# SBUF tiles on multiples of 256 bytes, and every row of the first norm weighted by one VectorE instruction, in a hybrid decoder layer

## The chip, the cores and the metric

The kernel runs on one core of one Trainium2 chip. The metric is the time of the program on the device, in microseconds (us), as the median of several runs. The engines are named as in the profile: PE is TensorE (PEld its weight loads), DVE is VectorE, ACT is ScalarE, POOL is GpSimd, SP issues most DMAs. SBUF is the core's working memory, 128 partitions wide; an address here is the byte offset within a partition, and a tile's *residue* is its address modulo 256.

## The reference

One decoder layer over 1024 tokens of width 1024, in float32. What matters here:

```
n = rmsnorm(x, mix_norm_w)                 # x * rsqrt(mean(x*x) + eps) * w, row by row
p = n @ w_in                               # columns: z | x B C | dt | q | k | v
y_s = gated SSD scan of (z, xBC, dt)       # convolution, chunked scan, silu(z) gate
y_a = differential attention of (q, k, v)
h = x + concat(y_s, y_a) @ w_out
h = h + (silu(n2 @ w_gate) * (n2 @ w_up)) @ w_down,  n2 = rmsnorm(h)
out = rmsnorm(h)
```

## The kernel before

**Products.** A large product is made of three PE passes: each operand is split into a high part (rounded to float32r by ACT) and a low part (the rest, by DVE), in `split` (L170 to L176) for weights and in `norm_transpose` (L113 to L124) for the normed rows. `mm3` (L126 to L129) issues hi\*hi, hi\*lo and lo\*hi into one PSUM tile, so each step of a product is three matmuls on lines 127, 128 and 129. The first operand of a matmul is the stationary one (its 128 columns are loaded as weights), the second the moving one (it streams through, 256, 264 or 512 columns here).

**First norm.** The 1024 tokens are eight blocks of 128 rows, t = 0 to 7. For each, `norm_rows` (L94 to L111) lets ACT square the row and sum it up (L99), DVE makes the mean (`ms_n`, L89), POOL raises it to the power -0.5 (`rs_n`, L91), and then the row is weighted: for even t by one DVE instruction with two SBUF tensors and a column (L111: x times rs times the norm's weight `mixw`); for odd t, POOL multiplies x by `mixw` (L108) and ACT scales it by `rs` (L109). PE then transposes the block in two halves of four (L120, `pt_n`, two PSUM buffers in pool SC), ACT rounds each half to `nhi` (L123), and DVE subtracts to get `nlo` (L124). A later transpose into the same PSUM buffer waits for that subtraction.

**First product.** `gate_dt` projects the 16 columns of dt and the first 512 of the gate z in two passes of 264 columns (a = 0 and 1; `proj_z0`, L258 to L266). Each pass has its weights in two units of four blocks of 128 rows, `wr_z` (as loaded), `wh_z` and `wl_z` (its parts), [128, 4, 264]. `wr` has two buffers, `wh` and `wl` three each, all in pool `wp`, in slots as large as the largest tile of each: 4 * 264 * 4 = 4,224 bytes, which is 16.5 times 256.

**Placement.** Pools follow one another in SBUF: `const` (its last tile is `pcol`, 69 columns), `small`, `big` (`nhi`, `nlo`, later operands), `wp`, `a4`, `p4`, `hx`, `ob`, `cv`, `sp`. In the built program `big` begins at 18,144, which is 224 modulo 256. From there on each tile's size is a multiple of 256 except in `wp`, so that `big`, `a4`, `p4`, `hx`, `ob` and `cv` are all at residue 224. The eight slots of `wp` alternate: `wr` 224 and 96, `wh` 224, 96, 224, `wl` 96, 224, 96. Every big tile is thus at 32 modulo 64.

**Order.** The kernel is recorded by a tile framework whose scheduler orders the instructions of each engine and inserts the waits; only one stretch of the FFN has its PE order fixed by hand. SP's loads are issued in its order, and each that reuses a buffer waits for that buffer's last reader.

**What follows.** After the first product: the projections with 512 moving columns (`proj_T`: B, C, x, q and k, 28 of them, each two halves of 24 matmuls), the SSD scans, attention, the output projection (256 columns), gate and up (11 pairs of column tiles, two matrices, seven products of 12 matmuls each; the stationary parts `wa` are in the `wh` and `wl` slots), and the down projection (11 pairs of row tiles, seven products of 12 matmuls; there both the stationary `dg` and the moving `dw` are in those slots).

Of the kernel before, what the change touches and what calls it, by code (L numbers as in the profile page):

```python
# [9 lines left out]
F32 = mybir.dt.float32  # L10
F32R = mybir.dt.float32r
# [6 lines left out]
P = 128  # L18
# [6 lines left out]
def tile_hybrid_block(  # L25
# [56 lines left out]
    nc.vector.memset(mhalf, -0.5)  # L82
    pcol = const.tile([P, 69], F32, name="pcol")
    CW, CB, SN, SL = 0, 48, 60, 68
# [9 lines left out]
    def norm_rows(parts, wbc, outs, name, pool=(), junk=None):  # L94
        """outs = RMSNorm of the row whose column pieces are parts; pieces in pool are weighted on Pool and scaled on ACT"""
        n, w = len(parts), DM // len(parts)
        ss = small.tile([P, n], F32, tag="ss1", name="ss_" + name)
        for i, p in enumerate(parts):
            nc.scalar.activation(outs[i] if junk is None else junk, p, AF.Square, accum_out=ss[:, i:i + 1])  # L99
        if n > 1:  # L100
            s1 = small.tile([P, 1], F32, tag="ss1", name="st_" + name)
            nc.vector.tensor_tensor(s1, ss[:, 0:1], ss[:, 1:2], op=ALU.add)
            ss = s1
        r = rstd_of(ss, DM, name)
        for i, (p, o) in enumerate(zip(parts, outs)):
            wi = wbc[:, i * w:i * w + w]
            if i in pool:
                nc.gpsimd.tensor_tensor(o, p, wi, op=ALU.mult)  # L108
                nc.scalar.mul(o, o, r)  # L109
            else:  # L110
                nc.vector.scalar_tensor_tensor(o, p, r, wi, op0=ALU.mult, op1=ALU.mult)  # L111
# [51 lines left out]

# [1 line left out]
    def load_raw(src, shape, name):  # L165
# [12 lines left out]
    w_in_k = w_in2.rearrange("(k p) c -> p k c", p=P)  # L178

    def z0_raw(a, u):  # L180
        """columns of dt and of the gate of group 0: 264 of 528"""
        raw = wp.tile([P, 4, 264], F32, tag="raw", bufs=2, name=f"wr_z0_{a}_{u}")
        k = slice(4 * u, 4 * u + 4)
        if a == 0:
            nc.sync.dma_start(raw[:, :, 0:16], w_in_k[:, k, C_DT:C_DT + 16])
            nc.sync.dma_start(raw[:, :, 16:264], w_in_k[:, k, C_Z:C_Z + 248])
        else:
            nc.sync.dma_start(raw, w_in_k[:, k, C_Z + 248:C_Z + 512])
        return raw

    def z0_unit(raw, a, u):
        hi = wp.tile([P, 4, 264], F32R, tag="wh", bufs=3, name=f"wh_z0_{a}_{u}")
        lo = wp.tile([P, 4, 264], F32R, tag="wl", bufs=3, name=f"wl_z0_{a}_{u}")
        split(hi, lo, raw)
        return hi, lo

# [1 line left out]
    xs = []  # L198
    mixw = P4([P, DM], F32, "mixw")
    for t in range(NT):  # L200
        xt = A4([P, DM], F32, f"x_{t}")
        nc.sync.dma_start(xt, x2[t * P:(t + 1) * P, :])
        xs.append(xt)
        if t == 0:
            nc.sync.dma_start(mixw, mix_norm_w[0].partition_broadcast(P))
        if t == 2:
            zraw = [z0_raw(0, u) for u in range(2)]
    nhi = [B16([P, KD, 512], f"nhi{i}") for i in range(2)]
    nlo = [B16([P, KD, 512], f"nlo{i}") for i in range(2)]
    for t in range(NT):  # L210
        norm_transpose([xs[t]], mixw, nhi, nlo, t, (CV if t % 2 else P4)([P, DM], F32, f"xm_{t}"), SC, f"n{t}",
                       (0,) if t % 2 else ())
        if t == 2:
            zus = [z0_unit(zraw[u], 0, u) for u in range(2)]

# [1 line left out]
    prow = P4([69, P], F32, "prow")  # L217
# [5 lines left out]
    nc.tensor.transpose(pps, prow, ident[:69, :69])  # L223
    nc.vector.tensor_copy(pcol, pps)
    nc.vector.tensor_scalar(pcol[:, SL:SL + 1], pcol[:, SL:SL + 1], 1.0 - LAMBDA_INIT, None, op0=ALU.mult)
# [9 lines left out]

# [1 line left out]
    def w_unit(src, shape, name, alloc=None):  # L237
# [10 lines left out]
    def proj_T(*jobs):  # L248
        """each job: a weight, a column, a name and sink(half, psum [128 columns, 512 tokens])"""
        us = [w_unit(w_k[:, :, col:col + P], [P, KD, P], name) for w_k, col, name, _ in jobs]  # L250
        for half in range(2):
            for (hi, lo), (_, _, name, sink) in zip(us, jobs):
                ps = MM([P, 512], f"mm_{name}_{half}")
                for k in range(KD):
                    mm3(ps, hi[:, k, :], lo[:, k, :], nhi[half][:, k, :], nlo[half][:, k, :], k == 0, k == KD - 1)
                sink(half, ps)

    def proj_z0(us, name, sink):  # L258
        """units of 264 columns; sink(t, psum [128 tokens, 264])"""
        for t in range(NT):  # L260
            ps = (MS if t % 4 > 1 else MM)([P, 264], f"mm_{name}_{t}")
            tk = slice((t % 4) * P, (t % 4) * P + P)
            for k in range(KD):
                hi, lo = us[k // 4]
                mm3(ps, nhi[t // 4][:, k, tk], nlo[t // 4][:, k, tk], hi[:, k % 4, :], lo[:, k % 4, :],
                    k == 0, k == KD - 1)  # L266
            sink(t, ps)

    def proj_nat(col, name, sink):
        """256 columns; sink(t, psum [128 tokens, 2 blocks from t, 256])"""  # L270
        us = [w_unit(w_in_k[:, 4 * u:4 * u + 4, col:col + 256], [P, 4, 256], f"{name}_{u}") for u in range(2)]
# [9 lines left out]

# [1 line left out]
    W16 = [P, NT, 16]  # L283
# [49 lines left out]

# [1 line left out]
    def conv_tiles(*tiles):  # L335
# [21 lines left out]
    def gate_dt():  # L357
        """the gate of group 0 and dt"""
        for a in range(2):
            zt = [None]  # L360
            w0, w = (0, 248) if a == 0 else (248, 264)

            def sink(t, ps):
                if t % 2 == 0:
                    zt[0] = CV([P, 2, w], F32, f"zt0_{a}_{t}")
                if a == 0:
                    nc.vector.tensor_tensor(adt[:, t, :], ps[:, 0:16], hv[:, 0, :], op=ALU.add)
                nc.scalar.activation(zt[0][:, t % 2, :], ps[:, 264 - w:], AF.Silu)
                if t % 2 == 1:
                    nc.gpsimd.dma_start(z_d[t - 1:t + 1, :, w0:w0 + w].rearrange("t p c -> p t c"), zt[0])  # L370
            proj_z0(zus if a == 0 else [z0_unit(z0_raw(1, u), 1, u) for u in range(2)], f"z0_{a}", sink)

# [138 lines left out]

# [1 line left out]
    cneg = sp.tile([P, P], F32, tag="cs", name="cneg")  # L513
# [13 lines left out]
    def v_pair(hh):  # L527
        # [head][block] views of the two heads; in the last pair but one, the heads' tiles are freed one by one
        by_head = hh == NH // 2 - 2
# [129 lines left out]

# [1 line left out]
    KG = 4  # L661
# [14 lines left out]
    def out_block(t, kys, ws, name, bank=MM):  # L676
        """two token blocks from t, 256 columns"""
        ps = bank([P, 2, 256], f"po_{name}_{t}")
# [47 lines left out]

# [1 line left out]
    # gate and up by Winograd's seven products: A are two column tiles by two halves of the contraction, B the two  # L728
    # halves of the contraction by two halves of the tokens; C = A B is summed up in PSUM (X, Y and Z)
    ORDER = (1, 2, 6, 5, 7, 3, 4)  # L730
# [4 lines left out]
    def room(p, early):  # L735
        """an operand B: [hi or lo][block of 128 rows] views of 512 tokens"""
        if early:
# [59 lines left out]
    def ffn_pair(pr, raws, order=ALL, ybank=SC):  # L797
        """silu(gate) * up of two column tiles; they and their sums as operands of the down projection to g_d"""
        sg, tm, c22, reg, sm = {}, {}, {}, [{}, {}], [{}, {}]
# [145 lines left out]
    def final_half(t, nh, last):  # L945
        """the first half of a row to be ready is weighted before its scale is known"""
        ho = h_parts(ho_all, t)
# [12 lines left out]

    # down, by the same seven products: A are the two halves of the tokens by two row tiles, B the row tiles by two
    # halves of the columns
    SLOT = {2: 0, 4: 1, 1: 2, 7: 3, 5: 4, 6: 5, 3: 6}
# [28 lines left out]
    for gi, prs in enumerate(groups):  # L992
# [5 lines left out]
        def psums(two, name):  # L998
            """four banks: one for each block of 128 tokens of a half"""
            if two:  # L1000
# [81 lines left out]
```

## Time and profile before

| What | Value |
|---|---|
| Median of 3 runs | 1642.38 us (1641.95 to 1642.83) |
| Profiled execution, span | 1643.3 us |
| PE busy | 1597.2 us (97%), 9170 matmuls |
| DVE busy | 1071.6 us (65%) |
| ACT busy | 775.8 us (47%) |
| POOL busy | 429.2 us (26%) |
| PE's first instruction | 8.33 us after the span's start |

The profile is of one execution; no time of its own is listed for that execution beside its span. The span lies 0.9 us above the median of the runs, so differences are worked out on the span and taken off the median. In a row of the timeline the columns are start, duration, engine, line, operation, and output<-inputs; matmuls are pipelined, so their pace is read from the starts, not from the durations.

### The profile page before, as it was taken

What the parts mean: (1) busy time and instruction counts of PE and PEld (TensorE: products, weight loads), DVE (VectorE), ACT (ScalarE), POOL (GpSimd) and SP (SyncE); (2) the same over time, 40 slices, a digit from 0 to 9 for tenths busy, and PEclk for the clock granted to TensorE, in tenths of its full rate; (3) what the DMA queues carried; (4) which work ended last, traced back from release to release, by engine and by line L of the source; (5) the groups of instructions that cost most, each with busy time, mean ns of one, the idle gap of its engine ahead of it and who ended that gap; (6) DMA issues with size and microseconds to landing.
All of it is one profiled execution on the core that took longest, in us unless ns stands there. A gap on an engine that the chain in (4) does not pass through costs nothing. (4 is left out here: it accounts for less than half of the span.)

```text
span 1643.3 us, 23716 instructions
## 1 busy us (share of the span) xinstructions
PE 1597.2 (97%) x9170; PEld 1386.9 (84%) x9170; DVE 1071.6 (65%) x1682; ACT 775.8 (47%) x1608; POOL 429.2 (26%) x378
## 2 busy tenths in 40 slices
PE   6999999999999999999999998999999999999997
PEld 6988878887989989889999987888888888778885
DVE  5345745688776676677674477455555555898987
ACT  6444764456555565575552245333333333334445
POOL 4100330032000000013300034444444443542322
PEclk9999999999999999999999999999999999999999
DMA  5321451143011110147523221233333323944122
GB/s 195 110 79 52 129 163 56 36 142 92 24 46 39 46 33 27 45 130 229 162 77 116 84 99 56 96 102 104 111 116 118 98 96 134 365 166 186 39 103 103
DMA packets 105291, 172.78 MB, mean 105 GB/s; under 512 B 7813, under 2 KB 75530, under 8 KB 103770
## 3 DMA queue, kind: packets, MB, share of 16 engines
q1 hardware_dynamic: 95210, 137.11, 25.2%
q0 software_dynamic: 9968, 34.15, 6.3%
q8 instruction: 72, 1.18, 0.3%
q14 instruction: 41, 0.34, 0.1%
HBM read 125.82 MB, written 45.42 MB: 104 GB/s over the span
## 5 line engine op out<-in xcount | busy, mean ns | idle before, releaser
L127 PE MATMUL x<-n,wa 128*128 128x512 f32 x352 | 138.7, 396 | 0.0
L128 PE MATMUL x<-n,wa 128*128 128x512 f32 x352 | 138.7, 394 | 0.0
L129 PE MATMUL x<-n,wa 128*128 128x512 f32 x352 | 137.8, 394 | 0.0
L590 ACT ACTIVATE p<-s,nmx 128x256 f32<-128x256 f32 (+7 forms) x128 | 94.4, 740 | 53.2 <-DVE nmx L588 49.9
L172 ACT CAST wa<-s 128x512 fp32r<-128x512 f32 x88 | 54.7, 622 | 132.3 <-PE x L129 59.4
L173 DVE TENSOR_TENSOR wa<-s,wa 128x512 fp32r<-128x512 f32 x88 | 76.8, 873 | 51.1 <-ACT wa L172 50.8
L172 ACT CAST dg<-gd 128x512 fp32r<-128x512 f32 x77 | 47.7, 620 | 114.7 <-PE dx L129 57.2
L588 DVE TENSOR_REDUCE nmx<-s 128x1 f32<-128x256 f32 (+7 forms) x128 | 95.3, 754 | 2.4
L173 DVE TENSOR_TENSOR dg<-gd,dg 128x512 fp32r<-128x512 f32 x77 | 66.2, 862 | 23.3 <-ACT dg L172 23.2
L129 PEld LDWEIGHTS x<-n,wa 128*128 128x128 f32 x352 | 66.5, 189 | 15.1
L128 PEld LDWEIGHTS x<-n,wa 128*128 128x128 f32 x352 | 66.6, 189 | 14.8
L127 PEld LDWEIGHTS x<-n,wa 128*128 128x128 f32 x352 | 66.6, 189 | 14.8
L127 PE MATMUL mm_z<-wh_z,nhi 128*128 128x264 f32 (+1 forms) x256 | 75.9, 298 | 2.3 <-ACT wh_z L172 2.3
L611 PE MATMUL o<-v,p 128*128 128x128 f32 x576 | 77.7, 275 | 0.0
L129 PE MATMUL mm_z<-wh_z,nlo 128*128 128x264 f32 (+1 forms) x256 | 77.3, 303 | 0.0
L611 PEld LDWEIGHTS o<-v,p 128*128 128x128 f32 x576 | 73.5, 191 | 2.7
L128 PE MATMUL mm_z<-wl_z,nhi 128*128 128x264 f32 (+1 forms) x256 | 75.0, 294 | 0.0
L127 PE MATMUL mm_v<-wh_v,nhi 128*128 128x256 f32 x256 | 74.2, 290 | 0.0
L129 PE MATMUL mm_v<-wh_v,nlo 128*128 128x256 f32 x256 | 74.1, 290 | 0.0
L128 PE MATMUL mm_v<-wl_v,nhi 128*128 128x256 f32 x256 | 73.5, 287 | 0.0
L128 PE MATMUL po_a<-wl_wo,yh 128*128 128x256 f32 x256 | 72.6, 283 | 0.0
L91 POOL TENSOR_TENSOR rs_o<-ms_o,mhalf 128x4 f32<-128x4 f32 x16 | 18.0, 1125 | 208.4 <-DVE ms_o L89 208.3
(331 smaller groups left out, 5172.9 us busy)
## 6 DMA issues: line engine op xcount, KB each, us to landing
gd<-g_d SPq DMA_DIRECT2D x11, 1792.0 KB, 7.8
wr_g<-in_w_gate_dram SPq DMA_DIRECT2D x22, 512.0 KB, 3.8
wr_u<-in_w_up_dram SPq DMA_DIRECT2D x22, 512.0 KB, 4.3
g_d<-sg SPq DMA_DIRECT2D x22, 512.0 KB, 5.1
wr_d<-in_w_down_dram SPq DMA_DIRECT2D x22, 512.0 KB, 5.0
L<-cs_d POOLq DMA_DIRECT2D x16, 512.0 KB, 4.4
wr_y<-yT_d SPq DMA_DIRECT2D x16, 512.0 KB, 3.8
wr_wo<-in_w_out_dram SPq DMA_DIRECT2D x16, 512.0 KB, 3.5
```

What stands on the lines that cost most here:

```text
L91: nc.gpsimd.tensor_tensor(r, ms, mhalf[:, :w], op=ALU.pow)
L127: nc.tensor.matmul(ps, lh, rh, start=first, stop=False, skip_group_check=more)
L128: nc.tensor.matmul(ps, lh, rl, start=False, stop=False, skip_group_check=more)
L129: nc.tensor.matmul(ps, ll, rh, start=False, stop=last, skip_group_check=more)
L172: nc.scalar.copy(hi, raw)
L173: nc.vector.tensor_tensor(lo, raw, hi.bitcast(F32), op=ALU.subtract)
L588: nc.vector.reduce_max(nmx[:, m:m + 1], s[:, :Lk], axis=AX.X, negate=True)
L590: nc.scalar.activation(p[:, :Lk], s[:, :Lk], AF.Exp, bias=nmx[:, m:m + 1], accum_out=sm[:, m:m + 1])
L611: nc.tensor.matmul(o, wT[:, j * P:(j + 1) * P], vt[h % 2][j], start=(j == 0), stop=(j == i))
```

## The change

Three things are changed.

1. `pcol` has 77 columns in place of 69. Nothing uses the eight more; they move all pools behind `const` up by 32 bytes. `big` now begins at 18,176, a multiple of 256.
2. The two passes of the first product are cut otherwise: pass 0 has 272 columns (dt's 16 and 256 of the gate) and three units of 3, 3 and 2 blocks of rows; pass 1 has 256 columns and two units of 4 blocks. The largest tile of `wr`, `wh` and `wl` is now 4,096 bytes, so every slot of `wp`, and every tile of all later big pools, is at residue 0. `z_d` is written in two runs of 256 columns. Within pass 0 a block is 1,088 bytes, so its moving operands start at 0, 64 and 128 modulo 256. The third unit of pass 0 reuses the first one's `wr` buffer.
3. All eight rows of the first norm are weighted by DVE's one instruction (L111); POOL's multiplication (L108) and ACT's scaling (L109) are no longer called.

```
-    pcol = const.tile([P, 69], F32, name="pcol")
+    pcol = const.tile([P, 77], F32, name="pcol")
...
+    Z0 = ((272, (0, 3, 6, 8)), (256, (0, 4, 8)))
...
     def z0_raw(a, u):
-        raw = wp.tile([P, 4, 264], F32, tag="raw", bufs=2, name=f"wr_z0_{a}_{u}")
-        k = slice(4 * u, 4 * u + 4)
+        w, ks = Z0[a]
+        k = slice(ks[u], ks[u + 1])
+        raw = wp.tile([P, ks[u + 1] - ks[u], w], F32, tag="raw", bufs=2, name=f"wr_z0_{a}_{u}")
         if a == 0:
             nc.sync.dma_start(raw[:, :, 0:16], w_in_k[:, k, C_DT:C_DT + 16])
-            nc.sync.dma_start(raw[:, :, 16:264], w_in_k[:, k, C_Z:C_Z + 248])
-        else:
-            nc.sync.dma_start(raw, w_in_k[:, k, C_Z + 248:C_Z + 512])
+        nc.sync.dma_start(raw[:, :, w - 256:], w_in_k[:, k, C_Z + a * 256:C_Z + a * 256 + 256])
...
-            zraw = [z0_raw(0, u) for u in range(2)]
+            zraw = [z0_raw(0, u) for u in range(3)]
...
-        norm_transpose([xs[t]], mixw, nhi, nlo, t, (CV if t % 2 else P4)([P, DM], F32, f"xm_{t}"), SC, f"n{t}",
-                       (0,) if t % 2 else ())
+        norm_transpose([xs[t]], mixw, nhi, nlo, t, (CV if t % 2 else P4)([P, DM], F32, f"xm_{t}"), SC, f"n{t}")
...
-    def proj_z0(us, name, sink):
+    def proj_z0(us, w, name, sink):
+        ks = [k for u in us for k in u]
         for t in range(NT):
-            ps = (MS if t % 4 > 1 else MM)([P, 264], f"mm_{name}_{t}")
+            ps = (MS if t % 4 > 1 else MM)([P, w], f"mm_{name}_{t}")
...
-            w0, w = (0, 248) if a == 0 else (248, 264)
+            w = Z0[a][0]
...
-                    nc.gpsimd.dma_start(z_d[t - 1:t + 1, :, w0:w0 + w].rearrange("t p c -> p t c"), zt[0])
+                    nc.gpsimd.dma_start(z_d[t - 1:t + 1, :, a * 256:a * 256 + 256].rearrange("t p c -> p t c"), zt[0])
```

The file after it is one line longer from there on: L111 stays L111, L124 stays L124, later lines move by one to three.

The scheduler makes another order of the first 60 or so instructions of DVE. In the next piece, DVE's rows before from the split of the first product's second unit to the subtraction of block 2 (`xm` is a weighted row, `nlo` a block's low part, `wl_z` a unit's low part, `ms_n` the mean of a row; numbers are buffers):

```order
L173 TENSOR_TENSOR wl_z_0_1_210<-wr_z_0_1_121,wh_z_0_1_209 128x1056
L89 TENSOR_SCALAR ms_n_216<-ss_n_214 128x1
L124 TENSOR_TENSOR nlo_136<-pt_n_0_169,nhi_134 128x4x128
L124 TENSOR_TENSOR nlo_136<-pt_n_1_176,nhi_134 128x4x128
L89 TENSOR_SCALAR ms_n_239<-ss_n_237 128x1
L89 TENSOR_SCALAR ms_n_261<-ss_n_259 128x1
L111 SCALAR_TENSOR_TENSOR xm_236<-x_126,rs_n_241,mixw 128x1024
...
L89 TENSOR_SCALAR ms_n_306<-ss_n_304 128x1
L111 SCALAR_TENSOR_TENSOR xm_281<-x_130,rs_n_286,mixw 128x1024
L124 TENSOR_TENSOR nlo_136<-pt_n_0_191,nhi_134 128x4x128
L124 TENSOR_TENSOR nlo_136<-pt_n_1_198,nhi_134 128x4x128
```

And the same stretch of DVE now:

```order
L173 TENSOR_TENSOR wl_z_0_1_212<-wr_z_0_1_121,wh_z_0_1_211 128x816
L124 TENSOR_TENSOR nlo_139<-pt_n_0_171,nhi_137 128x4x128
...
L111 SCALAR_TENSOR_TENSOR xm_219<-x_127,rs_n_224,mixw 128x1024
L89 TENSOR_SCALAR ms_n_266<-ss_n_264 128x1
L111 SCALAR_TENSOR_TENSOR xm_241<-x_129,rs_n_246,mixw 128x1024
L111 SCALAR_TENSOR_TENSOR xm_263<-x_131,rs_n_268,mixw 128x1024
...
L124 TENSOR_TENSOR nlo_139<-pt_n_0_193,nhi_137 128x4x128
L89 TENSOR_SCALAR ms_n_310<-ss_n_308 128x1
L124 TENSOR_TENSOR nlo_139<-pt_n_1_200,nhi_137 128x4x128
L111 SCALAR_TENSOR_TENSOR xm_285<-x_133,rs_n_290,mixw 128x1024
L173 TENSOR_TENSOR wl_z_0_2_216<-wr_z_0_2_124,wh_z_0_2_215 128x544
```

Rows 3, 4 and 5 are now weighted ahead of block 2's subtraction, where it was row 4 and row 6 before; the split of the third unit comes after it.

On SP, the loads behind the eight rows and the small `hv` were, before (`wr_z_1` is a unit of pass 1, `prow` holds small parameters that PE transposes early):

```order
L188 DMA wr_z_1_0_573<-in_w_in_dram 128x4x264
L188 DMA wr_z_1_1_579<-in_w_in_dram 128x4x264
L218 DMA prow<-in_conv_w_dram 48x128
L219 DMA prow<-in_conv_b_dram 12x128
L220 DMA prow<-in_ssd_norm_w_dram 8x128
```

and are now:

```order
L188 DMA wr_z_0_2_124<-in_w_in_dram 128x2x16
L189 DMA wr_z_0_2_124<-in_w_in_dram 128x2x256
L189 DMA wr_z_1_0_576<-in_w_in_dram 128x4x256
L220 DMA prow<-in_conv_w_dram 48x128
L221 DMA prow<-in_conv_b_dram 12x128
L222 DMA prow<-in_ssd_norm_w_dram 8x128
L223 DMA prow<-in_subln_w_dram 1x128
L189 DMA wr_z_1_1_582<-in_w_in_dram 128x4x256
```

The third unit's two loads stand ahead of `prow`, and the second unit of pass 1 behind it. Behind the start, PE's order is the same; DVE has one pair of neighbours exchanged in the FFN.

More of the change, by code (lines that the diff above doesn't have):

```diff
@@ L178, in tile_hybrid_block @@
     w_in_k = w_in2.rearrange("(k p) c -> p k c", p=P)
+    Z0 = ((272, (0, 3, 6, 8)), (256, (0, 4, 8)))
     def z0_raw(a, u):
-        raw = wp.tile([P, 4, 264], F32, tag="raw", bufs=2, name=f"wr_z0_{a}_{u}")
-        k = slice(4 * u, 4 * u + 4)
+        w, ks = Z0[a]
+        k = slice(ks[u], ks[u + 1])
+        raw = wp.tile([P, ks[u + 1] - ks[u], w], F32, tag="raw", bufs=2, name=f"wr_z0_{a}_{u}")
         if a == 0:
             nc.sync.dma_start(raw[:, :, 0:16], w_in_k[:, k, C_DT:C_DT + 16])
-            nc.sync.dma_start(raw[:, :, 16:264], w_in_k[:, k, C_Z:C_Z + 248])
-        else:
-            nc.sync.dma_start(raw, w_in_k[:, k, C_Z + 248:C_Z + 512])
+        nc.sync.dma_start(raw[:, :, w - 256:], w_in_k[:, k, C_Z + a * 256:C_Z + a * 256 + 256])
         return raw
     def z0_unit(raw, a, u):
-        hi = wp.tile([P, 4, 264], F32R, tag="wh", bufs=3, name=f"wh_z0_{a}_{u}")
-        lo = wp.tile([P, 4, 264], F32R, tag="wl", bufs=3, name=f"wl_z0_{a}_{u}")
+        w, ks = Z0[a]
+        shape = [P, ks[u + 1] - ks[u], w]
+        hi = wp.tile(shape, F32R, tag="wh", bufs=3, name=f"wh_z0_{a}_{u}")
+        lo = wp.tile(shape, F32R, tag="wl", bufs=3, name=f"wl_z0_{a}_{u}")
         split(hi, lo, raw)
-        return hi, lo
+        return [(hi[:, k, :], lo[:, k, :]) for k in range(shape[1])]
     xs = []
@@ L210, in tile_hybrid_block @@
     for t in range(NT):
-        norm_transpose([xs[t]], mixw, nhi, nlo, t, (CV if t % 2 else P4)([P, DM], F32, f"xm_{t}"), SC, f"n{t}",
-                       (0,) if t % 2 else ())
+        norm_transpose([xs[t]], mixw, nhi, nlo, t, (CV if t % 2 else P4)([P, DM], F32, f"xm_{t}"), SC, f"n{t}")
         if t == 2:
-            zus = [z0_unit(zraw[u], 0, u) for u in range(2)]
+            zus = [z0_unit(zraw[u], 0, u) for u in range(3)]
     prow = P4([69, P], F32, "prow")
@@ L223, in tile_hybrid_block @@
     nc.tensor.transpose(pps, prow, ident[:69, :69])
-    nc.vector.tensor_copy(pcol, pps)
+    nc.vector.tensor_copy(pcol[:, :69], pps)
     nc.vector.tensor_scalar(pcol[:, SL:SL + 1], pcol[:, SL:SL + 1], 1.0 - LAMBDA_INIT, None, op0=ALU.mult)
@@ L256, in proj_T @@
                 sink(half, ps)
-    def proj_z0(us, name, sink):
+    def proj_z0(us, w, name, sink):
+        ks = [k for u in us for k in u]
         for t in range(NT):
-            ps = (MS if t % 4 > 1 else MM)([P, 264], f"mm_{name}_{t}")
+            ps = (MS if t % 4 > 1 else MM)([P, w], f"mm_{name}_{t}")
             tk = slice((t % 4) * P, (t % 4) * P + P)
[L263 to L266, printed above, removed]
+            for k, (hi, lo) in enumerate(ks):
+                mm3(ps, nhi[t // 4][:, k, tk], nlo[t // 4][:, k, tk], hi, lo, k == 0, k == KD - 1)
             sink(t, ps)
@@ L360, in gate_dt @@
             zt = [None]
-            w0, w = (0, 248) if a == 0 else (248, 264)
+            w = Z0[a][0]
             def sink(t, ps):
                 if t % 2 == 0:
-                    zt[0] = CV([P, 2, w], F32, f"zt0_{a}_{t}")
+                    zt[0] = CV([P, 2, 256], F32, f"zt0_{a}_{t}")
                 if a == 0:
                     nc.vector.tensor_tensor(adt[:, t, :], ps[:, 0:16], hv[:, 0, :], op=ALU.add)
-                nc.scalar.activation(zt[0][:, t % 2, :], ps[:, 264 - w:], AF.Silu)
+                nc.scalar.activation(zt[0][:, t % 2, :], ps[:, w - 256:], AF.Silu)
                 if t % 2 == 1:
-                    nc.gpsimd.dma_start(z_d[t - 1:t + 1, :, w0:w0 + w].rearrange("t p c -> p t c"), zt[0])
-            proj_z0(zus if a == 0 else [z0_unit(z0_raw(1, u), 1, u) for u in range(2)], f"z0_{a}", sink)
+                    nc.gpsimd.dma_start(z_d[t - 1:t + 1, :, a * 256:a * 256 + 256].rearrange("t p c -> p t c"), zt[0])
+            proj_z0(zus if a == 0 else [z0_unit(z0_raw(1, u), 1, u) for u in range(2)], w, f"z0_{a}", sink)
     def gate(g):
```

## The prediction

> **What bounds the kernel now.** The page comes first: how long, and which engine is never idle.
>
> ```profile
> span 1643.3 us, 23716 instructions
> PE 1597.2 (97%) x9170; PEld 1386.9 (84%) x9170; DVE 1071.6 (65%) x1682; ACT 775.8 (47%) x1608; POOL 429.2 (26%) x378
> ```
>
> Only 46.1 us are without PE. The table of stages (stretch, its length, each engine's busy time with count, granted clock, DMA share, GB/s) tells where they lie:
>
> ```profile
> 0.00:20.00 20.00, 8.90 (x43) 8.20 (x44) 8.77 (x16) 13.67 (x21) 8.94 (x14) 1.00 0.94 314
> 20.00:40.00 20.00, 16.01 (x121) 15.59 (x120) 13.10 (x20) 11.84 (x21) 9.68 (x8) 0.91 0.24 73
> 40.00:60.00 20.00, 20.00 (x167) 20.00 (x167) 10.26 (x23) 10.13 (x16) 1.65 (x3) 1.00 0.30 92
> 1000.00:1600.00 600.00, 595.57 (x2590) 484.14 (x2589) 387.51 (x506) 218.30 (x378) 251.22 (x172) 1.00 0.36 127
> ```
>
> PE idles 11.1 + 4.0 us in the first 40 us and hardly at all later. So two things can shorten this kernel: fewer waits of PE in the first 40 us, or a quicker pace of its matmuls anywhere. The change touches both. PE's waits at the start, from the list of waits (total, times, longest):
>
> ```profile
> PE pt_n L120 <- DVE xm L111: 8.3, 1, 8.3
> PE pt_n L120 <- DVE nlo L124: 3.9, 1, 3.9
> PE mm_z L127 <- ACT wh_z L172: 2.3, 1, 2.3
> ```
>
> The 8.3 us are the first loads, which the change leaves alone. The 3.9 us are the place to read; PE's timeline there:
>
> ```profile
> 22.09 0.29 PE L127 MATMUL mm_z<-wh_z,nhi 128*128 128x264 f32 x1
> 22.21 0.28 PE L128 MATMUL mm_z<-wl_z,nhi 128*128 128x264 f32 x1
> ...
> 24.11 0.28 PE L128 MATMUL mm_z<-wl_z,nhi 128*128 128x264 f32 x1
> 28.27 0.66 PE L120 MATMUL pt_n<-ident,xm 128*128 128x128 f32 x4 [3.88 <-DVE nlo L124]
> ...
> 29.39 0.42 PE L127 MATMUL mm_z<-wh_z,nhi 128*128 128x264 f32 x1
> 29.61 0.42 PE L128 MATMUL mm_z<-wl_z,nhi 128*128 128x264 f32 x1
> ...
> 33.69 0.60 PE L120 MATMUL pt_n<-ident,xm 128*128 128x128 f32 x4
> ```
>
> Before the wait a matmul starts every 0.12 us; after it, every 0.22 us for a while, though the granted clock in that stage is 0.91: a wait is paid for twice. Block 3's transposes stood still because DVE had not yet subtracted block 2. DVE's and POOL's timelines say why:
>
> ```profile
> 6.99 1.28 DVE L111 SCALAR_TENSOR_TENSOR xm<-x,rs_n,mixw 128x1024 f32<-128x1024 f32 x1 [0.67 <-POOL rs_n L91]
> 9.22 0.15 DVE L89 TENSOR_SCALAR ms_n<-ss_n 128x1 f32<-128x1 f32 x1 [0.95 <-ACT xm L99]
> 13.89 2.42 DVE L173 TENSOR_TENSOR wl_z<-wr_z,wh_z 128x1056 fp32r<-128x1056 f32 x2
> 19.61 3.42 DVE L111 SCALAR_TENSOR_TENSOR xm<-x,rs_n,mixw 128x1024 f32<-128x1024 f32 x1 [0.77 <-POOL rs_n L91]
> 24.26 3.36 DVE L111 SCALAR_TENSOR_TENSOR xm<-x,rs_n,mixw 128x1024 f32<-128x1024 f32 x1 [0.80 <-POOL rs_n L91]
> 27.54 1.28 DVE L124 TENSOR_TENSOR nlo<-pt_n,nhi 128x512 fp32r<-128x512 f32 x2
> ```
>
> ```profile
> 6.40 0.55 POOL L91 TENSOR_TENSOR rs_n<-ms_n,mhalf 128x1 f32<-128x1 f32 x1 [5.03 <-DVE ms_n L89]
> 19.55 2.40 POOL L108 TENSOR_TENSOR xm<-x,mixw 128x1024 f32<-128x1024 f32 x1
> 24.19 2.35 POOL L108 TENSOR_TENSOR xm<-x,mixw 128x1024 f32<-128x1024 f32 x1
> 26.48 1.54 POOL L91 TENSOR_TENSOR rs_n<-ms_n,mhalf 128x1 f32<-128x1 f32 x1
> ```
>
> The same DVE instruction takes 1.28 us alone and 3.4 us where POOL multiplies a row: 2.35 or 2.40 us of POOL and then about 1 us of its own. The two exclude each other, in both directions: POOL's tiny `rs_n` takes 0.55 us alone, 1.54 us beside DVE's L111.
>
> **Part 1: the start.** Removed: four POOL multiplications, four ACT scalings, and two collisions on DVE (3.42 + 3.36 - 2 * 1.28 = 4.2 us). Added: four L111 on DVE at 1.28 us. DVE carries about as much as before, but in another order. I compare one point that PE passes with the same work done in both programs: block 4's first transposes, with 72 + 2 matmuls of pass 0 and blocks 0 to 3 behind them. Before, that is the row at 33.69. After, those transposes need the PSUM buffer that block 3's first subtraction frees, and DVE reaches that one after: seven L111 of rows 1 to 7 (7 * 1.28 = 9.0), three splits (816, 816 and 544 columns at 1.21 us per 1056: 2.5), seven subtractions (0.64 to 0.69 each: 4.6) and about a dozen small ones at 0.15 (1.8): 17.9 us. It can begin when row 1's `rs_n` is there, 9.22 + 0.15 + 0.55, about 10.0, and ends at 27.9. Against that, successive DVE instructions overlap by some 0.08 us (6.99 + 1.28 shows an end, 13.89 + 2.42 for two of 1.25 another), which takes 2 us off, and two `rs_n` that fall beside L111 put 2 * 1.0 on. So PE passes the point at 27 to 28.5, I take 28, against 33.69: 5.7 us less. PE itself can be there: 74 matmuls at 0.12 us are 9 us, and the 8 groups of four transposes at 0.6 (the row at 33.69) another 5; that fits between the first transposes at 8.3 and 28, with 6 us left for waits and the slow pace.
>
> What can take from this: the third unit. Its load waits on SP for the first split, done at about 13.8 on this chain (10.0 + 1.28 + 2 * 0.69 + 0.15 + 0.97), and stands behind the rows; the loads of that stage took
>
> ```profile
> x<-in_x_dram SPq DMA_DIRECT2D x8, 512.0 KB, 6.3
> wr_z<-in_w_in_dram SPq DMA_DIRECT2D x2, 528.0 KB, 7.2
> ```
>
> so with 7.2 us it is there at 21, before DVE comes to its split at about 25 (one L111, two subtractions and small rows stand between it and the point at 28). `prow`, which holds up PE at its transpose if late, stands behind 272 and 512 KB in place of two loads of 528 KB: no later than before. At the seam of the passes `wh_z_1_0` must wait for the third unit's buffers to turn over: ACT's rounding and DVE's subtraction (about 1.0 + 1.2) against 15 matmuls of 0.12 (1.8): 0.4 us lost. Columns are 272 + 256 for 264 + 264: nothing. Start: 5.7 - 0.4 = 5.3 us, between 2 (if PE stays at the 0.22 us pace through smaller waits) and 7.
>
> [...]
>
> **Part 2: the pace of all later matmuls.** Two neighbouring products of gate and up, on PE's timeline; both have the moving operand at residue 224, the first (z) its stationary one at 96, the second (x) at 224:
>
> ```profile
> 1117.83 0.40 PE L127 MATMUL z<-n,wa 128*128 128x512 f32 x1
> ...
> 1120.61 0.39 PE L128 MATMUL x<-n,wa 128*128 128x512 f32 x1
> 1120.83 0.39 PE L127 MATMUL x<-n,wa 128*128 128x512 f32 x1
> ...
> 1123.33 0.64 PE L129 MATMUL x<-n,wa 128*128 128x512 f32 x2
> ```
>
> Twelve steps in 2.78 us are 231.7 ns each; eleven in 2.50 are 227.3. Four products of the down projection (stationary, moving: 96, 96; 224, 224; 224, 96; and the next):
>
> ```profile
> 1472.24 0.63 PE L127 MATMUL dy<-dw,dg 128*128 128x512 f32 x2
> ...
> 1475.00 1.07 PE L127 MATMUL dx<-dw,dg 128*128 128x512 f32 x4
> ...
> 1477.73 1.09 PE L127 MATMUL dx<-dw,dg 128*128 128x512 f32 x4
> ...
> 1480.52 1.09 PE L127 MATMUL dx<-dw,dg 128*128 128x512 f32 x4
> ```
>
> Twelve steps each: 230.0, 227.5 and 232.5 ns. PE waits for nobody there; what differs is the placement. Pairs at one residue run at 227 to 230, mixed pairs at 232. And one half of an x projection, whose stationary parts alternate between a slot at 96 and one at 224:
>
> ```profile
> 129.15 0.39 PE L127 MATMUL mm_x<-nhi,wh_x 128*128 128x512 f32 x1
> ...
> 134.51 0.39 PE L129 MATMUL mm_x<-nhi,wl_x 128*128 128x512 f32 x1
> ```
>
> 23 steps in 5.36 us: 233.0 ns. After the change all of these pairs are at residue 0 on both sides, a pair that no row shows. The nearest is 224 with 224, also one residue on both sides: I take its 227.4. Then: gate and up, 11 * 2 * 7 * 12 = 1848 matmuls, half of them mixed: 924 * 4.3 ns = 4.0 us. Down, 11 * 7 * 12 = 924, a third of each kind: 308 * 2.6 + 308 * 5.1 = 2.4 us. Projections, 28 * 48 = 1344 at 5.6 at most, and I take 4.5, since in half of them the high part is the one at 224: 6.0 us. The 256-column products I put at nothing. Sum 12.4; a tenth I take off because where PE is quicker it will sometimes wait for ACT or DVE instead (it loses 4.4 us of 600 that way now): 11.2 us.
>
> From both sides: if one common residue is as bad as mixed pairs, 232.5 for all 4116, then the half that is now quicker loses: 924 * 5.1 + 308 * 5 + 308 * 2.5 = 7.0 us, less 0.5 ns of gain at 1344 (0.7): 6.3 us lost. If residue 0 also takes what 224 itself may cost, the gain can be larger. The stage from 40 to 60 has 167 instructions in 20.00 us, 120 ns each and nearly all of 264 columns; 227.4 ns for 512 columns leaves (227.4 - 120) / 248 = 0.433 ns a column and 5.7 ns a matmul that no column pays for. All of that gone would be 4116 * 5.7 = 23 us more.
>
> **Sum.** 1643.3 - 5.3 - 11.2 = 1626.8 on the span, which stands 0.9 above the median of 1642.4: 1626 us.
>
> **Rivals.**
> *Pace untouched.* The difference of 227 and 232 might hang on something else that alternates with the slots (which engine is writing the neighbouring slot). Then only the start counts: 1642.4 - 5.3 = 1637. [...] The rows above speak against it: same stage, same shapes, 4.4 ns. 12%.
> *Residue 0 better than 224.* What the misaligned start costs goes as well, half or all of the 5.7 ns: 12 to 23 us more than the forecast, 1603 to 1614. Against it: the first product's matmuls, whose moving blocks of 1,056 bytes step through the residues 224, 0, 32 and 64, run at one 0.12 us. 10%.
> *Slower: residue 0 is a bad pair.* Both operands then begin in the same place of SBUF, at a residue with the bit 128 clear, like 96, whose own pair (230.0) is already worse than 224's (227.5). If all 512-column matmuls took 235 ns, that is 4116 * 2.5 beyond the 6.3 above: 16.6 lost, 5.3 gained: 1654. It decides from a loss of 8.6 us, a common pace of about 233. 4%.
> *No gain at the start.* A late third unit or `prow` makes a new wait of 5 us in place of the old: 1631. 4%.
> Forecast: 70%, within itself 1619 to 1633.
>
> **How the numbers follow.** About 0.2% (3.3 us) is what a measurement of this kernel can tell from no change. Slower by more: the third rival, 4%. Within: the part of *Pace untouched* in which the start gives under 3.3 us, 4%. Faster: 92%. The range runs from 1614, which leaves out most of the second rival, to 1638, which takes in *Pace untouched*.
>
> **What would show it.** On DVE, eight L111 of about 1.28 us and no 3.4; PE's block 4 transposes at about 28 in place of 33.69, with no wait near 3.9 us; POOL without L108. In gate and up, twelve steps in 2.73 us in every product, and no alternation; in the projections 23 steps in about 5.25. Wrong would be: products at 2.78 throughout (residue 0 is like a mixed pair), at 2.60 or less (the misaligned start itself was the cost), a PE wait of several us on `wl_z` or `prow` before 30, or PE waits later that eat the pace.

## The result and the profile after

| | before | after |
|---|---|---|
| Median of 4 runs each | 1642.16 us (1641.70 to 1642.83) | 1624.95 us (1621.32 to 1630.94) |
| Ratio after / before | | 0.9897, 95% interval 0.9875 to 0.9918 |
| Span of the profiled execution | 1643.3 us | 1621.9 us |
| PE's first transposes of block 4 | 33.69 us | 27.87 us |

The kernel is 17.2 us faster; 1626 was forecast. The two spans differ by 21.4 us, which is too much: the profiled execution of after has a time of its own, 1623.63, 1.7 above its span and 1.3 below its median, and by the same 1.7 the span of before stands for about 1645.0, some 2.8 above its median. 21.4 less these 4.1 is 17.3, as the medians have it.

The page of after:

```profile
span 1621.9 us, 23723 instructions
PE 1582.6 (98%) x9170; PEld 1385.8 (85%) x9170; DVE 1074.5 (66%) x1687; ACT 772.2 (48%) x1605; POOL 420.1 (26%) x374
```

PE's matmuls are as many as before, and it is busy 14.6 us less: the pace is quicker, though a few of these us are stretches at half clock that this execution has fewer of (last section). The span shrank by more than that, so PE waits less too. The table of stages (busy time and count for PE, PEld, DVE, ACT, POOL; then granted clock, DMA share, GB/s):

```profile
0.00:20.00 20.00, 10.10 (x55) 9.70 (x56) 11.28 (x19) 13.98 (x24) 5.04 (x12) 1.00 0.92 317
20.00:40.00 20.00, 18.85 (x156) 18.63 (x155) 12.06 (x26) 9.43 (x20) 3.00 (x5) 1.00 0.17 58
1000.00:1600.00 600.00, 595.07 (x2615) 489.69 (x2614) 397.41 (x521) 222.02 (x383) 250.09 (x172) 1.00 0.35 127
```

In the first 40 us PE idles 9.9 + 1.15 = 11.05 us, 4.05 less than the 15.1 of before, and the granted clock from 20 to 40 is 1.00 where it was 0.91. Those 0.09 of 20 us are another 1.8: together 5.85, near the 33.69 - 27.87 = 5.82 of the table above. In the 600 us of the later stage PE has 25 matmuls more in the same time. PE's waits at the start (total, times, longest), and the transposes on its timeline:

```profile
PE pt_n L120 <- DVE ms_n L89: 3.0, 2, 1.9
PE mm_z L128 <- DVE wl_z L173: 0.2, 1, 0.2
```

```profile
11.87 1.12 PE L120 MATMUL pt_n<-ident,xm 128*128 128x128 f32 x4 [1.88 <-DVE ms_n L89]
...
22.05 0.66 PE L120 MATMUL pt_n<-ident,xm 128*128 128x128 f32 x4 [1.15 <-DVE ms_n L89]
...
27.87 0.60 PE L120 MATMUL pt_n<-ident,xm 128*128 128x128 f32 x4
```

The 3.9 us are gone, and so are the 2.3 on `wh_z`; two waits, of 1.88 and 1.15, stand in the stretch. The list puts both down to `ms_n`, the last thing that DVE did before; in the program both are for a subtraction (`nlo`). The second, at 22.05, is the old wait of block 3, shortened: DVE begins block 2's first subtraction at 21.36, where it was 27.54. On DVE's and POOL's timelines:

```profile
16.89 1.28 DVE L111 SCALAR_TENSOR_TENSOR xm<-x,rs_n,mixw 128x1024 f32<-128x1024 f32 x1
18.62 2.48 DVE L111 SCALAR_TENSOR_TENSOR xm<-x,rs_n,mixw 128x1024 f32<-128x1024 f32 x2 [0.38 <-POOL rs_n L91]
...
21.36 0.62 DVE L124 TENSOR_TENSOR nlo<-pt_n,nhi 128x512 fp32r<-128x512 f32 x1
...
23.76 0.72 DVE L173 TENSOR_TENSOR wl_z<-wr_z,wh_z 128x544 fp32r<-128x544 f32 x1
...
25.73 1.27 DVE L124 TENSOR_TENSOR nlo<-pt_n,nhi 128x512 fp32r<-128x512 f32 x2
```

```profile
16.31 2.79 POOL L91 TENSOR_TENSOR rs_n<-ms_n,mhalf 128x1 f32<-128x1 f32 x3 [3.81 <-DVE ms_n L89]
```

A weighted row takes DVE 1.28 us (2.48 for two), and none takes 3.4. The exclusion remains in the other direction: three `rs_n` beside the L111 at 16.89 take 2.79 us where three alone would take 1.65. The third unit's split (544 columns) is done at 24.48, and PE has no wait for it. The 0.2 us on `wl_z` in the list stand later, at 46.85, at the seam of the passes: the first unit of pass 1 comes a little late there.

The pace in gate and up, on PE's timeline; twelve steps lie between the first row and the second:

```profile
1102.76 0.39 PE L127 MATMUL z<-n,wa 128*128 128x512 f32 x1
...
1105.48 0.39 PE L128 MATMUL x<-n,wa 128*128 128x512 f32 x1
```

2.72 us, 226.7 ns a step, where the same z product took 231.7. In the down projection twelve steps lie between the two rows:

```profile
1452.52 0.62 PE L127 MATMUL dy<-dw,dg 128*128 128x512 f32 x2
...
1455.24 1.07 PE L127 MATMUL dx<-dw,dg 128*128 128x512 f32 x4
```

226.7 ns again; before, the three kinds were 230.0, 227.5 and 232.5. And 24 steps of an x projection:

```profile
121.89 0.39 PE L129 MATMUL mm_x<-nhi,wl_x 128*128 128x512 f32 x1
...
127.33 0.39 PE L129 MATMUL mm_x<-nhi,wl_x 128*128 128x512 f32 x1
```

5.44 us, 226.7 ns, against 233.0. But the 256-column products went the other way. The output projection, before (20 steps) and after (44 steps):

```profile
853.55 0.28 PE L129 MATMUL po_a<-wh_wo,yl 128*128 128x256 f32 x1
...
855.91 0.28 PE L128 MATMUL po_a<-wl_wo,yh 128*128 128x256 f32 x1
```

```profile
850.82 0.28 PE L129 MATMUL po_a<-wh_wo,yl 128*128 128x256 f32 x1
...
856.09 0.28 PE L128 MATMUL po_a<-wl_wo,yh 128*128 128x256 f32 x1
```

2.36 / 20 is 118.0 ns, 5.27 / 44 is 119.8.

### The profile page after: what moved, and what is told of

Same layout as the page of the kernel before. It is cut to its first block, busy times and chain, and to the rows that moved or that the text cites. A ratio compares the mean times of both kernels' runs of the same rounds, so it can differ in the third digit from the quotient of the medians.

```text
span 1621.9 us, 23723 instructions
## 1 busy us (share of the span) xinstructions
PE 1582.6 (98%) x9170; PEld 1385.8 (85%) x9170; DVE 1074.5 (66%) x1687; ACT 772.2 (48%) x1605; POOL 420.1 (26%) x374
## 5 line engine op out<-in xcount | busy, mean ns | idle before, releaser
L129 PE MATMUL mm_z<-wh_z,nlo 128*128 128x256 f32 (+1 forms) x256 | 76.2, 298 | 0.0
L127 PE MATMUL mm_z<-wh_z,nhi 128*128 128x256 f32 (+1 forms) x256 | 75.1, 297 | 0.0
L128 PE MATMUL mm_z<-wl_z,nhi 128*128 128x256 f32 (+1 forms) x256 | 74.8, 293 | 0.2 <-DVE wl_z L173 0.2
```

Of the source, the lines that this page charges most:

```text
L127: nc.tensor.matmul(ps, lh, rh, start=first, stop=False, skip_group_check=more)
L128: nc.tensor.matmul(ps, lh, rl, start=False, stop=False, skip_group_check=more)
L129: nc.tensor.matmul(ps, ll, rh, start=False, stop=last, skip_group_check=more)
```

## The experiments

The table sets each trace against that of before at the same instruction of PE: how many us earlier it starts (the time at the left is that of before). It is worked out from the starts in the traces, and read with the section on the clock below: a jump of 1.7 us within a column is often one stretch at half clock. In before, gate and up run from 974 to 1414 us and down from there to 1633, so 1,606 of the 1,848 matmuls of gate and up lie between the rows 1024 and 1394.

| PE in before at | after | after, again | norm only | placement only | all at 224 | mixed |
|---|---|---|---|---|---|---|
| 35.6, block 4 | 5.9 | 5.9 | 5.1 | 2.9 | 4.3 | 4.3 |
| 60.4, in pass 1 | 5.2 | 5.2 | 5.1 | 2.3 | 3.6 | 3.7 |
| 1024, in gate and up | 13.4 | 8.6 | 10.2 | 6.3 | 7.4 | 9.4 |
| 1394, late in gate and up | 19.5 | 14.7 | 10.2 | 12.4 | 13.5 | 9.5 |
| 1600, late in down | 21.3 | 16.7 | 10.2 | 15.4 | 15.7 | 9.4 |

**After, again.** No edit.

> The changed kernel unedited, as the measure for the others on this chip: 0.9875 to 0.9918 of the kernel before, with the wide scatter of its first four runs (1621 to 1631 us) if that belongs to the kernel, or within 0.5% if it was chance.

1625.87 us (1624.86 to 1628.25), ratio 0.9899 [0.9886, 0.9913]. The result repeats; the wide scatter of the first four runs does not. Its trace is at 60 us as far ahead as the first one and 4.6 us less at the end; the difference arises between 60 and 1024, none of it between 1024 and 1394 (6.1 in both).

**The norm alone.** The kernel before, with this edit and nothing else:

```
-        norm_transpose(..., SC, f"n{t}",
-                       (0,) if t % 2 else ())
+        norm_transpose(..., SC, f"n{t}")
```

> The kernel before with its odd rows weighted by DVE too; placement and units as before. If the two terms add up: the start's 5 to 6 us alone, a ratio of 0.9965 (about 1636.5 us), block 4's first transposes near 28 us, and twelve steps of gate and up still alternating between 2.73 and 2.78 us. If the start's gain needs the new cut into three units: less than 3 us. If the pace came from the new order and not from the placement: products without alternation and 15 us or more.

1637.65 us, ratio 0.9965 [0.9953, 0.9977]: 5.4 us less than the 1643.05 of before on that chip. PE's transposes in its trace, block 3's first half and block 4's:

```profile
24.73 0.66 PE L120 MATMUL pt_n<-ident,xm 128*128 128x128 f32 x4 [0.52 <-DVE nlo L124]
...
28.59 0.60 PE L120 MATMUL pt_n<-ident,xm 128*128 128x128 f32 x4
```

The wait on `nlo` is 0.52 in place of 3.88, and block 4 begins at 28.59 with the old units and the old placement. The gain is there at 60 us, and in gate and up the trace gains nothing; there the z product that took 231.7 ns still does, by its twelve steps:

```profile
1107.59 0.40 PE L127 MATMUL z<-n,wa 128*128 128x512 f32 x1
...
1110.37 0.39 PE L128 MATMUL x<-n,wa 128*128 128x512 f32 x1
```

2.78 us, as before. Its column gains another 5.1 us between 60 and 1024, but not by pace: step by step its matmuls there take what they took, PE waits some 3.4 us less for ACT and DVE in the scans and attention, and it has one stretch at half clock less (1.7). The instructions of that part are those of before, so this is a difference of two executions, and the median of 5.4 doesn't have it. The norm's part is the start.

**The placement alone.** The changed kernel with the norm's argument put back:

```
+                       (0,) if t % 2 else ())
```

> The changed kernel with the odd rows weighted by POOL and scaled by ACT as before; placement at residue 0 and the three units stay. If the terms add up: the pace's 11 to 16 us alone, a ratio of 0.990 to 0.993 (about 1626 to 1631 us), with L111 of 3.4 us and a PE wait of some 4 us back at the start. If the three units are bad without the quicker norm: up to 3 us slower than that.

1628.69 us, ratio 0.9915 [0.9901, 0.9929], 14.4 us less than before. POOL multiplies again, and DVE and PE show it:

```profile
18.85 3.41 DVE L111 SCALAR_TENSOR_TENSOR xm<-x,rs_n,mixw 128x1024 f32<-128x1024 f32 x1 [0.38 <-POOL rs_n L91]
```

```profile
23.21 0.86 PE L120 MATMUL pt_n<-ident,xm 128*128 128x128 f32 x4 [1.85 <-DVE nlo L124]
...
30.69 0.60 PE L120 MATMUL pt_n<-ident,xm 128*128 128x128 f32 x4
```

One collision of L111 remains, with a wait of 1.85 on `nlo` (some 4 were expected), and block 4 begins at 30.69. DVE's split of 544 columns meets POOL too: it takes 2.69 us there, 0.72 in the changed kernel. Against 33.69, 3.0 us are won without the norm, by the new units and the placement that goes with them. The two parts of the change therefore overlap: 5.4 + 14.4 = 19.8 us of medians against 17.2 for both at once (after, again, on the same chip), and the overlap of 2.6 is about the 2.3 us that this kernel already has at 60 us.

**All at one residue, but not a multiple of 256.** The changed kernel with the old size of `pcol`, so that every big tile stands at 224:

```
-    pcol = const.tile([P, 77], F32, name="pcol")
+    pcol = const.tile([P, 69], F32, name="pcol")
```

> The changed kernel with pcol of 69 columns again: every big tile at residue 224, all the same, none on a multiple of 256. If what counts is that the stationary and the moving operand share a residue: as the changed kernel within 3 us (ratio 0.988 to 0.991), 512-column steps at 227 ns. If the multiple of 256 itself counts: steps of 229 ns or more and 5 to 12 us of the gain lost (ratio 0.993 to 0.997).

1625.87 us, ratio 0.9894 [0.9879, 0.9909]: the same as the changed kernel. Twelve steps of gate and up:

```profile
1101.04 0.39 PE L127 MATMUL z<-n,wa 128*128 128x512 f32 x1
...
1103.76 0.39 PE L127 MATMUL x<-n,wa 128*128 128x512 f32 x1
```

2.72 us, 226.7 ns again. The multiple of 256 brings nothing; the common residue brings the pace.

**Slots that alternate again.** The changed kernel with the `wh` and `wl` tiles of pass 1 eight columns wider, which makes those slots 4,224 bytes, so that they alternate between 0 and 128, while all other big tiles stay at 0:

```
-        hi = wp.tile(shape, F32R, tag="wh", ...)
-        lo = wp.tile(shape, F32R, tag="wl", ...)
+        hi = wp.tile([P, shape[1], w + 8 * a], F32R, tag="wh", ...)[:, :, :w]
+        lo = wp.tile([P, shape[1], w + 8 * a], F32R, tag="wl", ...)[:, :, :w]
```

> The changed kernel with the slots of wh and wl 4,224 bytes long again (tiles of pass 1 padded by 8 columns), so that they alternate between residue 0 and 128 while all other big tiles stay at 0. If sharing a residue is what counts: the pace's term is lost again, 512-column steps alternate between 227 and 232 ns, and the ratio is 0.995 to 0.998, the start's 5 to 6 us being left. If only residues off a multiple of 64 are bad: as the changed kernel (0.988 to 0.991).

1636.08 us, ratio 0.9962 [0.9949, 0.9975], what the norm alone gives. Twelve steps of a product with its stationary part at 128 and the moving one at 0:

```profile
1100.38 0.40 PE L127 MATMUL z<-n,wa 128*128 128x512 f32 x1
...
1103.18 0.40 PE L127 MATMUL x<-n,wa 128*128 128x512 f32 x1
```

2.80 us, 233 ns. In the table this trace gains nothing after 1024. With the order of all engines and the cut of the passes as in the changed kernel, 128 bytes of difference between the slots take the later gain away whole.

**Matmuls by themselves.** A kernel of matmuls only, on constant data (0.5) and run once, in products of 24 as the layer has them (hi\*hi, hi\*lo, lo\*hi). Four letters name a product: the residues of the stationary high and low part and of the moving high and low part, a for 0, b for 32, up to h for 224; W has 512 columns, N 256. Each product is issued twice, 48 steps.

> Leaves the layer out and computes nothing of it: products of 24 matmuls alone, no other engine at work, in two forms (512 columns, 256 columns), with the four operands (stationary high and low, moving high and low) at residues given by letters, a = 0, b = 32, ... h = 224 modulo 256. If the residue of the stationary operand against the moving one costs the 4 to 5 ns: 512-column steps of 227 ns where all four letters are equal, whatever the letter, and 231 to 235 where they differ; 256-column steps within 1 ns of 119 throughout. If the cost comes from other engines that write the neighbouring slots: all codes equal. If multiples of 256 or of 64 count by themselves: aaaa quicker than bbbb, dddd and hhhh.

The first row of a product and that of the next, for five products:

```profile
43.93 0.39 PE L70 MATMUL Waaaa<-arena 128*128 128x512 f32 x1
54.81 0.39 PE L70 MATMUL Waaae<-arena 128*128 128x512 f32 x1
...
76.78 0.39 PE L70 MATMUL Waaee<-arena 128*128 128x512 f32 x1
87.94 0.40 PE L70 MATMUL Waeaa<-arena 128*128 128x512 f32 x1
...
342.57 0.39 PE L70 MATMUL Whhhh<-arena 128*128 128x512 f32 x1
353.48 0.39 PE L70 MATMUL Whdhh<-arena 128*128 128x512 f32 x1
...
397.77 0.28 PE L70 MATMUL Naaaa<-arena 128*128 128x256 f32 x1
403.51 0.28 PE L70 MATMUL Naaae<-arena 128*128 128x256 f32 x1
...
511.53 0.28 PE L70 MATMUL Naagg<-arena 128*128 128x256 f32 x1
516.98 0.28 PE L70 MATMUL Naahh<-arena 128*128 128x256 f32 x1
```

All at 0: 10.88 / 48 = 226.7 ns. All at 224: 10.91 / 48 = 227.3. Stationary at 0, moving at 128: 11.16 / 48 = 232.5. All eight products with one letter lie between 226.7 and 227.6; of the 24 others the best has 228.8 and the worst 234.0. With 256 columns, where 119 throughout was expected, the sign turns: a common residue is among the slowest, 5.74 / 48 = 119.6, and a moving operand 192 bytes beyond the stationary one takes 5.45 / 48 = 113.5.

**The same in steps of 16 bytes.** Letters a to p are now 0 to 240.

```
-    R = {c: i * 8 for i, c in enumerate("abcdefgh")}
+    R = {c: i * 4 for i, c in enumerate("abcdefghijklmnop")}
```

> Leaves the layer out: matmuls alone again, with residues in steps of 16 bytes (a = 0, b = 16, ... m = 192, p = 240), mostly the moving operand against stationary ones at 0, and the other way round. If only the difference of the two residues counts: 256-column steps at 113 to 114 ns wherever the moving operand lies 192 beyond the stationary one (aamm, eeaa, ggcc) and 117 to 120 elsewhere; 512-column steps at 227 where the two are equal alone and 229 to 235 elsewhere. If the 113.6 of the first look was chance: 117 to 120 for aamm.

With 512 columns and the stationary part at 0, the moving one at 16 to 224 takes 229.1 to 234.5 ns; only 240 is as good as 0, with 226.8. With 256 columns two distances are quick, 112 bytes (113.3) and 192 (113.7), and all others take 116.7 to 120.0. For 512 columns the distance is what counts: products at one distance but other addresses agree within 0.3 ns (233.1 to 233.4 for four pairs 192 apart, 229.1 and 229.2 for two 64 apart). For 256 columns it is not all. The stationary part at 64 with the moving one at 0 is also 192 apart and quick, 5.45 us for 48 steps, and so is 192 with 128 (113.3 ns). But 96 with 32, which was expected to be quick as well, takes 5.65 us, 117.7 ns; its last nine steps, between the last two rows, take 1.06 us:

```profile
452.93 0.28 PE L70 MATMUL Neeaa<-arena 128*128 128x256 f32 x1
458.38 0.28 PE L70 MATMUL Nggaa<-arena 128*128 128x256 f32 x1
...
508.27 0.28 PE L70 MATMUL Nggcc<-arena 128*128 128x256 f32 x1
509.33 0.28 PE L70 MATMUL Nmmii<-arena 128*128 128x256 f32 x1
```

At a distance of 160 the two pairs tried differ too, 117.3 (0 with 160) and 120.1 (96 with 0).

**A version from this.** The kernel with all tiles at 224, with the stationary parts of the output projection 64 bytes further on, so that its moving operand is 192 beyond them:

```
-        yh, yl = B16([P, KG, T], f"yh{kg}"), B16([P, KG, T], f"yl{kg}")
+        yh, yl = [B16([P, KG * T + 64], f"y{e}{kg}")[:, 16:16 + KG * T].rearrange("p (k t) -> p k t", t=T) for e in "hl"]
```

> The changed kernel at residue 224 throughout (pcol 69), but the operand of the output projection that is stationary there moved up by 64 bytes in its slots, so that the moving one lies 192 beyond it in its 1536 matmuls of 256 columns; nothing else differs. If the difference of residues sets the step in the kernel as it does alone: these steps go from 119.7 to about 113.6 ns, 9 us less, a ratio of 0.983 to 0.986. If the step of 256 columns is set by other things in the kernel: no change from the 0.989 to 0.990 of the kernels with one residue.

1623.06 us, ratio 0.9877 [0.9857, 0.9896]. 18 steps of the output projection:

```profile
850.88 0.28 PE L127 MATMUL po_a<-wh_wo,yh 128*128 128x256 f32 x1
...
852.92 0.28 PE L127 MATMUL po_a<-wh_wo,yh 128*128 128x256 f32 x1
```

2.04 us, 113.3 ns, where the changed kernel has 119.8. The step is as expected, the total is not: 0.983 to 0.986 stood there. For the total it was run a second time, beside its own base on one chip:

> The kernel of po_shift once more, beside its own base on one chip. From the trace of its first run, 6 to 7 us less than the base between the output projection's start and gate and up: a ratio of 0.984 to 0.987 where the base has 0.988 to 0.990. If the shift is worth nothing at the end: both ratios within 0.001 of each other.

> The kernel of res224 once more, as the base for po_shift on this chip: 0.988 to 0.990 of the kernel before.

1622.23 us against 1627.82 (0.9873 [0.9855, 0.9892] against 0.9907 [0.9892, 0.9922]): 5.6 us. All 1,536 matmuls have the shift, and step by step in the traces those of 256 columns take 7.6 us less than with all at 224; the medians give less than that, but the intervals hold both. Both ratios lie above what was expected of them. It is the fastest of the kernels here; against the changed kernel itself it was not run on one chip, and by the ratios (0.9875 against 0.9898) the two are 3.8 us apart with intervals that overlap.

## Why the prediction was right, point by point

**The start, 5.3 us.** Right in cause, and in size for this trace: 5.8 at block 4's first transposes (27.87 where 28 stood), 5.2 left at 60 us (0.6 lost, 0.4 forecast). The cause is shown: the norm alone gives 5.1 of it. That 28 fitted so well is partly luck. The chain had DVE come last, with block 3's first subtraction ending at 27.9; DVE began it at 25.73 and had it by 26.4, and PE, without a wait since 22.05, came to the point later by its own work. The size also hangs on the clock. Five traces of the varied kernels above have the same instructions at the start: three of them have a stretch at half clock near 22 us and are 3.6 to 3.7 ahead at 60 us, and the two without are 4.5 and 5.0 ahead. And the forecast put the whole on the norm and the new units at nothing; the placement alone has 2.3 at 60 us, so the units would have taken part of the wait by themselves.

**Gate and up, 4.0 us.** Right in cause, too small: 6.8. Between the rows 1024 and 1394 every trace in the table with a common residue gains 6.1 on 1,606 of the 1,848 matmuls (13.4 to 19.5, 8.6 to 14.7, 6.3 to 12.4, 7.4 to 13.5), and the two without gain 0 and 0.1. The step that was mis-sized is "half of them mixed": the mixed half went from 232.8 to 226.8 on average over all its steps, 5.5 us, and the half that already had one residue went from 228.2 to 226.7 as well, 1.3 us. In the kernel before its products stand between mixed ones: its 121 steps next to a mixed one take 231.8 on average, the 804 others 227.7.

**Down, 2.4 us.** 1.7 and 1.9 in the two traces of the changed kernel, from its first matmul to its last. Right; the steps give 2.8 and 3.1, and some 1.1 of it goes into longer waits of PE on DVE, the loss for which the forecast took its tenth off.

**Projections, 6.0 us, and 256 columns, nothing.** Here the working failed twice, both times to the high side. Of the 1,368 three-pass steps of 512 columns ahead of 980 us, the 1,298 that take under 250 ns in both kernels went from 232.0 to 228.3 on average, 4.8 us. The step "the 256-column products I put at nothing" was wrong: 118.2 became 119.5, and 2,536 steps lose 3.2 us. The net is 1.6 where 6.0 stood. The forecast had read no row of a 256-column product, and their pace moves the other way.

**The sum.** By what was measured: 5.2 + 6.8 + 1.8 + 1.6 = 15.4 of 17.2, where 16.5 was forecast. Gate and up came out 2.8 above the forecast and the projections 4.4 below, so that the total fits better than its terms: that is luck. The rest is within the interval (0.9875 to 0.9918 is 13.5 to 20.5 us). The two traces differ by more, 21.4, and what lies beyond the 15.4 can be named: between 60 and 974 us the trace of before waits some 3.7 us longer for ACT and DVE and has one more stretch at half clock (1.6). The trace of the norm alone, whose instructions there are those of before, gains the same two, so they belong to the one execution of before that was profiled and not to the change.

**The rivals.** *Pace untouched* is out: the placement alone gives 14.4 us and the slots that alternate take it back. In the matmuls by themselves a step with the stationary operand at 0 takes 226.7 ns with the moving one at 0 and 232.5 with it at 128, and the two differ in nothing else. *Residue 0 better than 224* is out: 226.7 in both kernels, and 226.7 to 227.6 for every common residue by itself; the 5.7 ns a matmul aren't the price of a misaligned start. *Residue 0 is a bad pair* is out by the same rows, for 512 columns; for 256 columns a common residue is in fact nearly the worst. *No gain at the start* is out: PE has no wait for the third unit. Whether the multiple of 256 does anything for the loads at the start can't be seen: a row's load took 7.1 us in after and 7.2 with all at 224, longer in both than the 6.3 of before, and PE begins at 8.03 in after, but at 8.36 with the placement alone, which has the same alignment, and at 8.26 with all at 224.

## What to carry to other kernels

Where PE is the bound, read its pace from the starts of neighbouring products of one shape: 2% between two of them that differ only in where their operands lie (231.7 and 227.3 ns in gate and up before) is a gain that no list of waits shows, and placing is free. Then measure each shape that the kernel uses before one placement is chosen for all, since a common residue was best for 512 columns here (226.7 ns a step, 232.5 with the moving operand 128 bytes on) and nearly the worst for 256 (119.6, and 113.5 with it 192 bytes on). And a helper engine that took half of a row-wise job was no help here, where its work shut out the engine it relieved: 2.4 us of POOL cost DVE 2.1 (an L111 of 3.4 us in place of 1.28).

## What the runs showed of the hardware

**The distance of two operands.** For these three-pass float32r products, a 512-column step takes 226.7 to 227.6 ns when stationary and moving operands begin at one residue modulo 256, and 228.8 to 234.5 at other distances but 240 bytes (226.8). A 256-column step takes 119.6 to 120.0 at one residue and 116.7 to 120.1 otherwise, but 113.3 to 113.7 in all products tried in which the moving operand is 112 or 192 bytes beyond the stationary one, except one (96 with 32, 117.7). One thing more does not fit: before, the products of the down projection with both operands at 96 took 230.0 ns in the kernel, where a common residue of 96 by itself takes 227.2. That placement sets the pace is shown; why the distance matters, and what was different in these two cases, is open.

**Half clock after a wait.** The granted clock falls to 0.50 for 3.4 us after some waits of PE, and not after others. The first two rows are of before; the next two of after, the first of them at the place in the program where before has its second; the last three of after's second trace:

```profile
29.10:32.50 3.40, 3.40 (x18) 3.40 (x17) 1.76 (x3) 1.75 (x3) 0.00 (x0) 0.50 0.32 77
223.70:227.10 3.40, 3.40 (x12) 2.37 (x11) 2.97 (x6) 2.02 (x3) 1.29 (x2) 0.51 0.24 96
```

```profile
216.30:220.00 3.70, 3.70 (x23) 3.08 (x24) 3.63 (x6) 2.68 (x5) 1.29 (x2) 1.00 0.34 97
980.00:983.40 3.40, 3.40 (x9) 2.63 (x8) 3.40 (x6) 2.53 (x6) 2.77 (x3) 0.50 0.00 0
```

```profile
217.70:221.10 3.40, 3.40 (x12) 2.37 (x11) 2.91 (x6) 1.77 (x3) 1.29 (x2) 0.51 0.36 108
378.20:381.60 3.40, 3.40 (x11) 2.73 (x10) 3.17 (x6) 1.30 (x2) 1.47 (x2) 0.50 0.62 207
982.30:989.10 6.80, 6.16 (x19) 4.81 (x20) 6.80 (x9) 3.80 (x9) 6.09 (x5) 0.50 0.04 7
```

The first row is the slow pace behind the wait of 3.88 us, and its price, half of 3.4 us, is the 1.7 that the start of after won beside the waiting itself. Up to 1000 us the trace of before has three such stretches, that of after one of 3.4 us, its repetition four: 5.1 us by price, and the spans of the last two differ by 4.6. So one and the same kernel scatters by such stretches, and a difference of two profiles by a few us says nothing until they are counted.

The length of a wait does not decide alone. In before a wait of 2.13 us that ends at 223.1 is followed by a stretch; in the trace of the norm alone one of 2.11 at the same place is not; in after's repetition one of 1.1 us that ends at 377.3 is. What the traces show is a grid: within each of the ten traces of the layer the starts of the stretches differ by whole multiples of 3.413 us (in before they are 29.071, 223.630 and 991.629, which are 57.0 and 225.0 such steps apart), and the grid lies otherwise in each trace (carried back to the span's start, its first point is at 1.76 us in before and at 0.36 in after). The slow pace at PE's first matmuls ends on the same grid: a step takes 220 ns up to 18.83 us in before and 227 up to 17.42 in after, then about 122 and 125; the first stretch begins 3.0 grid steps later in before and 282.0 later, at 979.98, in after. The clock records begin only at these two times, so that the 1.00 of the stage from 0 to 20 does not tell of it.

Where a wait lies on the grid thus differs from one execution to the next. That this is why the same wait brings a stretch in one and not in the other is the author's guess; no run shows it.
